# Four PSUM banks for the scores, and the second block's transposes behind the second block's scores, in an attention and Fourier encoder

## The chip, the cores and the metric

The kernel runs on one core of one Trainium2 chip. The metric is device time in microseconds (us), the median of the runs that are given. The engines are named as in the profile: PE multiplies matrices (PEld is its weight load), DVE, ACT and POOL work on vectors, SP issues most transfers. PE writes its results into PSUM, which has eight banks of 2 KB in each of 128 partitions; DVE and ACT read them from there.

## The reference

Two sequences, a prompt of 2048 tokens and a sample of 512, go through two layers and a last normalisation. All of it is float32.

```python
def attention_layer(x, g, w_in, w_out, sink, rel_bias):
    h = rmsnorm(x, g)
    z = h @ w_in                      # q (16 heads of 64), k and v (4 heads), gate
    ...
    o = banded_gqa_with_sink(q, k, v, rel_bias, sink)
    return x + (o * jax.nn.silu(gate)) @ w_out

def banded_gqa_with_sink(q, k, v, rel_bias, sink):
    # blocks of 128 queries against the block before, its own and the one behind (384 keys)
    scores = jnp.einsum('bnqhgd,bnkhd->bnhgqk', qb, kw) * scale + bias
    scores = jnp.where(mask, scores, -jnp.inf)
    ...
    p = jnp.exp(scores - m)
    p = p / (jnp.sum(p, axis=-1, keepdims=True) + jnp.exp(sk - m))
    return jnp.einsum('bnhgqk,bnkhd->bnqhgd', p, vw)

def fourier_layer(x, g, w_gate, w_out):
    f = jnp.fft.fftn(hg, axes=(1, 3), norm="ortho").real   # positions and the channels of a group
    return x + (f * jax.nn.silu(h @ w_gate)) @ w_out
```

## The kernel before

**Numbers.** Each float32 operand of a large product is split into a high and a low part, and a product is three matmuls (`matmul3`, L91 to L94): high by high, high by low, low by high. So nearly every result that PE makes is read twice after it: ACT copies the high part (CAST or COPY), DVE subtracts it from the value to get the low part.

**Chunks.** Attention runs over five chunks of 512 tokens: the sample (called chunk 0 here, `c` in the code), then the four quarters of the prompt (1 to 4). For each chunk `kv_proj` (L299) makes keys (`kwin`) and values (`v`; `vp` is their PSUM bank), with `kh` the keys of one neighbouring block (`halo`), transposed in `kht`. Then a loop of 17 steps, n = 0 to 16 (L842), goes over eight pairs of heads and, for each pair, two pairs of query blocks: step n works at head pair n//2 and blocks 2(n%2) and the next, which are called the first and the second block below. A block at an end of its sequence has 256 keys, any other 384.

**One step.** For the new pair of blocks there are six score matmuls for each block: two heads j = 0 and 1, on the two halves of PE's rows, three products each (`scores`, L467). DVE adds the bias and takes the minimum into SBUF (`biased`, L486, a custom instruction), ACT takes exponentials (`exps`, L494), DVE and ACT divide. For the old pair, that of step n-1, PE transposes the weights of attention, eight or twelve transposes of 64 rows for a block (`transp`, L525), their two halves h = 0 and 1 going into two banks `pt`; ACT and DVE copy them into high and low parts (`parts`, L533 and L534); and PE multiplies them by v (`av`, L551). Between these stand quotas of the projections of q (`qp`) and gate (`gp`) for later heads, and from step 14 on of the output projection (`op`, in `out_proj`). The tile `s` is the gate times its tanh (L414), read from `gp`'s bank, so it frees that bank.

**What sets the order.** The code writes the order of the step by hand. Instructions that go through `pe` or `seq` (L139 to L146) are chained in that order on PE, DVE and ACT; everything else is placed by the scheduler of the tile framework, and an engine runs its instructions strictly in the resulting order. A tile that reuses a bank waits for the last reader of the tile that had it. The diff therefore also moves some instructions that it doesn't mention.

**Banks.** There are eight. Five rotate under the name `bank` (L76) for everything but the scores: pt, av, qp, gp, vp, op, ib. Three fixed ones, spt0 to spt2 (L278), take the scores: the first block's two heads go to spt0 and spt1, the second block's to spt2 and spt0. At step 0 a rotating bank (`fourth`, L840) stands in for the second use of spt0. The first half of the output projection uses spt0 to spt2 and one rotating bank, the second half four rotating ones. The Fourier phase opens a second pool of three banks where the score banks were.

Of the kernel before, what the change touches and what calls it, by code (L numbers as in the profile page):

```python
# [9 lines left out]
F32 = mybir.dt.float32  # L10
# [32 lines left out]
def encoder(  # L43
# [10 lines left out]
    dram = ctx.enter_context(tc.tile_pool(name="dram", bufs=1, space=DRAM))  # L54
    psum = ctx.enter_context(tc.tile_pool(name="psum", bufs=5, space=PSUM))

# [19 lines left out]
    def bank(name):  # L76
        return psum.tile([P, 512], F32, tag="bank", name=name)

# [69 lines left out]
    def attention_phase():  # L148

        with ExitStack() as es:  # L150
# [127 lines left out]
            spt = []  # L278
            for i in range(3):
                spt.append(spsum.tile([P, 512], F32, name=f"spt{i}"))  # L280
# [18 lines left out]
            def kv_proj(c, hs, halo, norms=None, early=None):  # L299
# [33 lines left out]
                if halo:  # L333
                    ps = bank(f"kh{c}")[:, :256]
                    for k in range(KD):
                        matmul3(ps, halo[k], wslice(wk, k, 0, 256), k == 0, k == KD - 1)
                    kh = ap.tile([P, 256], F32, tag="tmp", bufs=2, name=f"kh{c}")
                    ACT.copy(kh, ps)
# [33 lines left out]
                if halo:  # L372
                    pt = bank(f"kht{c}")[:, :256]
                    for t in range(2):
                        PE.transpose(pt[:, t * P : t * P + P], kh[:, t * P : t * P + P], ident)
                        evac_k(t, pt[:, t * P : t * P + P], P, CH + P)
                for t in range(3):
                    zeros(spt[t])
# [50 lines left out]
            def attention(c, p, res, uTs):  # L429
# [82 lines left out]
                def transp(b):  # L512

                    gb, k0, k1 = span(b)
                    ss = [st.pop((b, j)) for j in range(2)]
                    if b % 2 == 0:
                        st["pts"] = ap.tile([P, 2, 2, 3, 2, P], F32R, align_bytes=LINE, tag="pt", bufs=1, name=f"pts{c}_{p}_{b}")
                    ps = st["pt", b] = [
                        bank(f"pt{c}_{p}_{b}_{h}")[:, :384].rearrange("p (k j q) -> p k j q", k=3, j=2) for h in range(2)
                    ]  # L520
                    for j in range(2):
                        for kb in range(k0, k1):
                            for h in range(2):
                                rows = slice(64 * h, 64 * h + 64)
                                pe(PE.transpose(  # L525
                                    ps[h][:, kb, j, :], ss[j][rows, 1 + kb * P : 1 + (kb + 1) * P], ident[rows, rows]
                                ))
# [57 lines left out]
            def out_proj(c, uTs):  # L585
# [4 lines left out]
                def mm(half, k, tiles):  # L590
                    if k == 0 and 3 in tiles:

                        st["ps"] = (spt if half == 0 else []) + [bank(f"op{c}_{half}_{i}") for i in range(3 * (1 - half), 4)]
                    if k % 2 == 0 and 3 in tiles:
# [188 lines left out]
            for c in range(len(CHUNKS)):  # L783
# [55 lines left out]

                fourth = bank(f"s{c}")  # L840
                zeros(fourth)
                for n in range(17):  # L842
# [15 lines left out]
                    if old:  # L858
                        for b in range(2):
                            old[0].transp(old[1] + b)  # L860
                    if new:
                        for j in range(2):
                            new[0].biased(new[1], j)
                        new[0].scores(new[1] + 1, (spt[2], spt[0] if n else fourth))
                    if n == 15:
# [50 lines left out]
    def fourier_phase(tail):  # L916
        with ExitStack() as es:
            fp = es.enter_context(tc.tile_pool(name="four", bufs=1, reuse_waits="tile"))
            psum2 = es.enter_context(tc.tile_pool(name="psum2", bufs=3, space=PSUM, reuse_waits="tile"))

# [272 lines left out]
            for i, s in enumerate(tail):  # L1193
# [7 lines left out]
                if 1 <= i < 9:  # L1201
                    w, k = split_steps[i - 1]
                    take(ready[w, k], k, left, *{"T": ("T2", "T1"), "B": ("B11", "B22")}[w])
            wstack.close()
            zp = es.enter_context(tc.tile_pool(name="zp", bufs=1, side="right", reuse_waits="tile"))

# [567 lines left out]
```

## Time and profile before

| | |
|---|---|
| time, median of 3 runs | 1594.49 us (1594.38 to 1595.07) |
| span of the profiled execution | 1592.8 us |
| its own time beside the span | not listed; the runs lie 1.6 to 2.3 us above this span |
| PE busy | 1581.6 us, 99% |
| PE weight load busy | 1319.4 us, 83% |
| DVE busy | 1145.4 us, 72% |
| ACT busy | 871.7 us, 55% |
| POOL busy | 447.5 us, 28% |

A row of the timeline has the start in us from the start of the span, the length from the first start to the last end in the row, the engine, line, operation, output and inputs, and the count; what stands in brackets at its end is idle time before it. Matmuls overlap, and their ends are modelled, so an engine that waits between two short matmuls is still shown as busy. A stall of PE must be read from the starts of its rows, and from the length of a group against that of a like group.

### The profile page before, as it was taken

Reading aid. Unit: us, or ns where it says so; the run is one execution under the profiler, and the core shown is the slowest. Engines: PE = TensorE matmul, PEld = TensorE weight load, DVE = VectorE, ACT = ScalarE, POOL = GpSimd, SP = SyncE. Lnnn points to the kernel's source line nnn. Section 1 sums busy time; section 2 is a strip of 40 time slices with the busy share of each in tenths; the row PEclk is TensorE's granted clock in tenths of the full one; section 3 lists DMA queues with packets and bytes.
Section 4 is the critical chain, followed back from the end, with each engine's and each line's share of the span. In section 5 each row is a group of like instructions: output and inputs, shape, how many; then the busy total and the mean of one; then the engine's idle time right before and its main releaser. Section 6 shows DMA issues by size and latency. Waiting matters only on the chain. (4 is left out here: it accounts for less than half of the span.)

```text
span 1592.8 us, 27377 instructions
## 1 busy us (share of the span) xinstructions
PE 1581.6 (99%) x9743; PEld 1319.4 (83%) x9743; DVE 1145.4 (72%) x2785; ACT 871.7 (55%) x2088; POOL 447.5 (28%) x613
## 2 busy tenths in 40 slices
PE   9999999999999999999999999999999999999998
PEld 7888888888888888988888888888888888888886
DVE  6788655776547785377764577669778778989896
ACT  6688534776246684257752476646655554343342
POOL 2475642421404314024223242223112111101110
PEclk9999999999999999999999999999999999999999
DMA  7597695566856567656649655675666569557762
GB/s 295 198 342 271 221 361 209 205 235 210 299 208 214 209 235 252 240 198 226 236 168 327 225 205 207 234 255 210 212 209 238 185 218 406 182 186 299 274 207 79
DMA packets 100579, 373.88 MB, mean 235 GB/s; under 512 B 12139, under 2 KB 22379, under 8 KB 83036
## 3 DMA queue, kind: packets, MB, share of 16 engines
q1 hardware_dynamic: 81708, 297.91, 53.0%
q0 software_dynamic: 16400, 70.04, 11.5%
q10 hardware_dynamic: 2336, 4.20, 0.7%
q8 instruction: 77, 1.26, 0.3%
q14 instruction: 58, 0.48, 0.1%
HBM read 280.84 MB, written 91.26 MB: 234 GB/s over the span
## 5 line engine op out<-in xcount | busy, mean ns | idle before, releaser
L486 DVE CUSTOM_DVE_ANT_0 S<-spt,b 128x385 f32<-128x385 f32 (+1 forms) x315 | 154.2, 528 | 128.7 <-PE spt L467 80.2
L94 PE MATMUL gp<-h,wg 128*128 128x512 f32 x960 | 237.4, 395 | 0.0
L94 PE MATMUL qp<-h,wq 128*128 128x512 f32 x960 | 237.0, 396 | 0.0
L533 ACT CAST pts<-pt 128x384 fp32r<-128x384 f32 (+1 forms) x320 | 123.5, 473 | 176.2 <-PE pt L525 176.1
L94 PEld LDWEIGHTS gp<-h,wg 128*128 128x128 f32 x960 | 174.9, 188 | 43.3 <-issue 9.7
L94 PEld LDWEIGHTS qp<-h,wq 128*128 128x128 f32 x960 | 174.9, 188 | 41.2 <-issue 5.5
L494 ACT ACTIVATE S<-S 128x385 f32<-128x385 f32 (+1 forms) x320 | 190.4, 606 | 20.4 <-DVE S L486 17.7
L534 DVE TENSOR_TENSOR pts<-pt,pts 128x384 fp32r<-128x384 f32 (+1 forms) x320 | 147.4, 523 | 21.2 <-ACT pts L533 21.2
L94 PE MATMUL op<-wo,uT 128*128 128x512 f32 x600 | 140.4, 391 | 0.0
L467 PE MATMUL spt<-kwin,qab 64*128 64x384 f32 (+1 forms) x945 | 132.3, 357 | 0.0
L94 PEld LDWEIGHTS op<-wo,uT 128*128 128x128 f32 x600 | 111.9, 188 | 23.9 <-issue 0.7
L575 POOL TENSOR_TENSOR uT<-o,uT 128x256 fp32r<-128x256 f32 x75 | 55.5, 740 | 244.9 <-ACT uT L574 240.6
L551 PEld LDWEIGHTS av<-pts,v 128*128 128x128 f32 x576 | 101.4, 188 | 18.7
L551 PE MATMUL av<-pts,v 128*128 128x512 f32 (+1 forms) x576 | 115.7, 341 | 0.0
L94 PE MATMUL fo<-wo,tTu 128*128 128x512 f32 x480 | 115.2, 392 | 0.0
L467 PEld LDWEIGHTS spt<-kwin,qab 64*128 64x128 f32 x945 | 85.8, 185 | 31.1 <-issue 24.7
L94 PEld LDWEIGHTS fo<-wo,tTu 128*128 128x128 f32 x480 | 88.4, 188 | 17.0
L506 DVE TENSOR_SCALAR S<-S 128x384 f32<-128x384 f32 (+1 forms) x192 | 90.4, 471 | 6.4
L571 POOL TENSOR_TENSOR o<-o,s 128x256 f32<-128x256 f32 x75 | 55.2, 736 | 134.5 <-DVE o L569 134.3
L94 PE MATMUL spt<-wo,uT 128*128 128x512 f32 x360 | 86.7, 392 | 0.0
L94 PEld LDWEIGHTS spt<-wo,uT 128*128 128x128 f32 x360 | 66.5, 188 | 13.7
L525 PEld LDWEIGHTS pt<-ident,S 64*128 64x128 f32 x1792 | 68.0, 138 | 3.7 <-issue 1.8
(321 smaller groups left out, 3030.2 us busy)
## 6 DMA issues: line engine op xcount, KB each, us to landing
wo<-wsd SPq DMA_DIRECT2D x32, 1024.0 KB, 5.7
wq<-wsd SPq DMA_DIRECT2D x31, 1024.0 KB, 7.5
wg<-wsd SPq DMA_DIRECT2D x31, 1024.0 KB, 5.1
x<-x1d SPq DMA_DIRECT2D x40, 512.0 KB, 3.8
b<-b21d SPq DMA_DIRECT2D x40, 512.0 KB, 6.5
b<-rowd SPq DMA_DIRECT2D x40, 384.0 KB, 4.2
xs<-in_x_dram SPq DMA_DIRECT2D x23, 512.0 KB, 6.4
s2d<-gt POOLq DMA_DIRECT2D x40, 256.0 KB, 5.1
```

The source lines that it names most:

```text
L94: pe(PE.matmul(out, a[i], b[j], start=start and i + j == 0, stop=stop and i == 1, skip_group_check=more))
L467: pe(PE.matmul(banks[j][:, 2 + k0 * P : 2 + k1 * P], res["q"][rows, qp, b * P : (b + 1) * P], kwin[g][rows, kp, b * P + k0 * P : b * P + k ...
L486: seq(DVE, DVE.tensor_tensor_reduce(out=s[:, e0:e1], in0=ps[:, 1 + e0 : 1 + e1], in1=st["bias"][:, j, 386 - e1 : 386 - e0][:, ::-1], scale ...
L494: last_exp[0] = seq(ACT, ACT.activation(s[:, e0:e1], s[:, e0:e1], AF.Exp, bias=s[:, 386:387], scale=-1.0, accum_out=s[:, 387:388]))
L506: seq(DVE, DVE.tensor_scalar(s[:, ks], s[:, ks], den, None, ALU.mult))
L525: pe(PE.transpose(ps[h][:, kb, j, :], ss[j][rows, 1 + kb * P : 1 + (kb + 1) * P], ident[rows, rows]))
L533: seq(ACT, ACT.copy(hi, ps[:, k0:k1]))
L534: seq(DVE, DVE.tensor_tensor(lo, ps[:, k0:k1], f32(hi), ALU.subtract))
L551: pe(PE.matmul(to, v, pt, start=n == part == 0, stop=part == 1 and n in (1, len(todo) - 1), skip_group_check=n > 1,))
L571: eng.tensor_tensor(o, o, s, ALU.mult)
L575: low = eng.tensor_tensor(lo, o, f32(hi), ALU.subtract)
```

## The change

It does five things.

1. There are four score banks, spt0 to spt3, and four rotating ones. The second block's scores go to spt2 and spt3.
2. The old pair's second block is transposed behind the new second block's scores, no longer ahead of them. Its half h = 0 goes to a rotating bank, its half h = 1 into spt0 (columns 2 to 385), which the first block's scores of the same step have just used.
3. The halo's keys `kh` are projected into spt3 in place of a rotating bank.
4. The first half of the output projection uses one rotating bank, as its first tile, and spt1 to spt3; the second half three rotating banks and spt0.
5. The rotating pool is closed after the attention's tail, and in the Fourier phase a pool of five takes its place; until then the Fourier phase also has four.

The diff, without what only passes these on:

```diff
-    psum = ctx.enter_context(tc.tile_pool(name="psum", bufs=5, space=PSUM))
+    pstack = ctx.enter_context(ExitStack())
+    banks = [pstack.enter_context(tc.tile_pool(name="psum", bufs=4, space=PSUM))]
...
     def bank(name):
-        return psum.tile([P, 512], F32, tag="bank", name=name)
+        return banks[-1].tile([P, 512], F32, tag="bank", name=name)
...
-            for i in range(3):
+            for i in range(4):
                 spt.append(spsum.tile([P, 512], F32, name=f"spt{i}"))
...
                 if halo:
-                    ps = bank(f"kh{c}")[:, :256]
+                    ps = spt[3][:, :256]
...
-                    ps = st["pt", b] = [
-                        bank(f"pt{c}_{p}_{b}_{h}")[:, :384].rearrange("p (k j q) -> p k j q", k=3, j=2) for h in range(2)
-                    ]
+                    ps = [bank(f"pt{c}_{p}_{b}_{h}")[:, :384] for h in range(2 - b % 2)]
+                    if b % 2:
+                        ps.append(spt[0][:, 2:386])
+                    ps = st["pt", b] = [t.rearrange("p (k j q) -> p k j q", k=3, j=2) for t in ps]
...
-                        st["ps"] = (spt if half == 0 else []) + [bank(f"op{c}_{half}_{i}") for i in range(3 * (1 - half), 4)]
+                        own = [bank(f"op{c}_{half}_{i}") for i in range(3 if half else 1)]
+                        st["ps"] = own + spt[:1] if half else spt[1:] + own
...
-                fourth = bank(f"s{c}")
-                zeros(fourth)
...
                     if old:
-                        for b in range(2):
-                            old[0].transp(old[1] + b)
+                        old[0].transp(old[1])
                     if new:
                         for j in range(2):
                             new[0].biased(new[1], j)
-                        new[0].scores(new[1] + 1, (spt[2], spt[0] if n else fourth))
+                        new[0].scores(new[1] + 1, spt[2:])
+                    if old:
+                        old[0].transp(old[1] + 1)
...
-            psum2 = es.enter_context(tc.tile_pool(name="psum2", bufs=3, space=PSUM, reuse_waits="tile"))
+            psum2 = es.enter_context(tc.tile_pool(name="psum2", bufs=3, space=PSUM, side="right", reuse_waits="tile"))
...
             wstack.close()
+            pstack.close()
+            banks.append(es.enter_context(tc.tile_pool(name="psum3", bufs=5, space=PSUM, reuse_waits="tile")))
```

Three places of the order show what moves. In a name such as pt2_3_2_0_6578 the numbers are chunk, head pair, block and half, and a number that the build gives. The line numbers of the changed kernel are one or two higher.

The first place is PE at step 8 of chunk 2, with the scores of head pair 4 and the transposes of head pair 3. Before:

```order
L467 MATMUL spt0_227<-kwin_230,qab2_4_6534 128x384
L467 MATMUL spt1_228<-kwin_230,qab2_4_6534 128x384
...
L525 MATMUL pt2_3_2_0_6578<-ident_72,S2_3_2_0_6486 128x64
L525 MATMUL pt2_3_2_1_6579<-ident_72,S2_3_2_0_6486 128x64
...
L525 MATMUL pt2_3_3_0_6592<-ident_72,S2_3_3_0_6508 128x64
L525 MATMUL pt2_3_3_1_6593<-ident_72,S2_3_3_0_6508 128x64
...
L467 MATMUL spt2_229<-kwin_230,qab2_4_6534 128x384
L467 MATMUL spt0_227<-kwin_230,qab2_4_6534 128x384
...
L94 MATMUL gp2_4_6555<-h2_4_5150,wg2_4_6193 128x512 x3
```

The same place in the changed kernel:

```order
L468 MATMUL spt0_227<-kwin_231,qab2_4_6489 128x384
L468 MATMUL spt1_228<-kwin_231,qab2_4_6489 128x384
...
L527 MATMUL pt2_3_2_0_6533<-ident_72,S2_3_2_0_6428 128x64
L527 MATMUL pt2_3_2_1_6534<-ident_72,S2_3_2_0_6428 128x64
...
L468 MATMUL spt2_229<-kwin_231,qab2_4_6489 128x384
L468 MATMUL spt3_230<-kwin_231,qab2_4_6489 128x384
...
L527 MATMUL pt2_3_3_0_6557<-ident_72,S2_3_3_0_6463 128x64
L527 MATMUL spt0_227<-ident_72,S2_3_3_0_6463 128x64
...
L95 MATMUL gp2_4_6510<-h2_4_5115,wg2_4_6151 128x512 x3
```

The twelve transposes of the second block (3) now stand between the second block's scores and the projection, and their second half writes spt0.

The second place is PE at step 14 of chunk 2, where the output projection begins; the names in brackets are the engines and transfers that an instruction waits for. Before:

```order
L195 MATMUL ib3_4_7412<-ident_72,inv3_7172 128x128 [waits PE_49]
L94 MATMUL op2_0_3_7415<-wo2_0_0_7416,uT2_0_5574 128x512 [waits DMAHW0_49,PE_49]
L94 MATMUL op2_0_3_7415<-wo2_0_0_7416,uT2_0_5574 128x512 x2
L94 MATMUL op2_0_3_7415<-wo2_0_0_7416,uT2_1_5626 128x512 x3
L94 MATMUL op2_0_3_7415<-wo2_0_2_7424,uT2_2_5820 128x512 [waits DMAHW4_49]
```

The same place in the changed kernel:

```order
L196 MATMUL ib3_4_7360<-ident_72,inv3_7122 128x128 [waits PE_49]
L95 MATMUL op2_0_0_7363<-wo2_0_0_7364,uT2_0_5539 128x512 [waits DMAHW5_49,DVE_49]
L95 MATMUL op2_0_0_7363<-wo2_0_0_7364,uT2_0_5539 128x512 x2
L95 MATMUL op2_0_0_7363<-wo2_0_0_7364,uT2_1_5588 128x512 x3
L95 MATMUL op2_0_0_7363<-wo2_0_2_7372,uT2_2_5781 128x512 [waits DMAHW4_49]
```

The order is the same, but the first matmul of the output projection now waits for DVE: with four rotating banks it gets the bank of the last gate projection, which DVE frees when it writes `s` (L414). It is so in chunks 0, 1 and 2.

The third place is DVE in the steps 2, 6, 10 and 14 of chunks 1 to 3, here step 2 of chunk 2, where the last two blocks of one head's keys are copied to the front of `kwin` for the next chunk (L306), once the scores that read the front are done. Before:

```order
L534 TENSOR_TENSOR pts2_0_2_5827<-pt2_0_3_1_5843,pts2_0_2_5827 128x6x64
L486 ISA S2_1_1_0_5878<-spt2_229,b2_1_5624 128x385
...
L486 ISA S2_1_1_1_5880<-spt0_227,b2_1_5624 128x385
...
L502 RECIPROCAL S2_1_0_0_5856<-S2_1_0_0_5856 128x1
L306 CAST kwin_230<-kwin_230 128x2x256
L506 TENSOR_SCALAR S2_1_0_0_5856<-S2_1_0_0_5856 128x384
```

The same place in the changed kernel:

```order
L536 TENSOR_TENSOR pts2_0_2_5788<-pt2_0_2_1_5790,pts2_0_2_5788 128x6x64
L307 CAST kwin_231<-kwin_231 128x2x256
L536 TENSOR_TENSOR pts2_0_2_5788<-pt2_0_3_0_5813,pts2_0_2_5788 128x6x64
L536 TENSOR_TENSOR pts2_0_2_5788<-spt0_227,pts2_0_2_5788 128x6x64
L487 ISA S2_1_1_0_5838<-spt2_229,b2_1_5586 128x385
...
L487 ISA S2_1_1_1_5840<-spt3_230,b2_1_5586 128x385
```

The copy of the keys has moved up: it stands ahead of the copies of the second block's transposes and of the second block's biased scores, where it stood behind both.

More of the change, by code (lines that the diff above doesn't have):

```diff
@@ L376, in kv_proj @@
                         evac_k(t, pt[:, t * P : t * P + P], P, CH + P)
-                for t in range(3):
+                for t in range(4):
                     zeros(spt[t])
```

## Prediction

> **What bounds the kernel now.** I read the page's table of busy times first, then PE's waits, then the timeline of single steps, since the table cannot show a short stall.
>
> ```profile
> PE 1581.6 (99%) x9743; PEld 1319.4 (83%) x9743; DVE 1145.4 (72%) x2785; ACT 871.7 (55%) x2088; POOL 447.5 (28%) x613
> ...
> PE idle L239 <- DVE idle L236: 1.2, 1, 1.2
> PE W L94 <- DVE c L1136: 1.0, 1, 1.0
> ```
>
> PE is busy 99% of a span of 1592.8 us, and its longest visible waits are 1.2 and 1.0 us, once each. So PE is the bound, and what the change is worth must be sought inside the time in which PE counts as busy. One step of chunk 3 (n = 4), PE first, then DVE:
>
> ```profile
> 715.03 0.78 PE L467 MATMUL spt<-kwin,qab 64*128 64x384 f32 x6
> 715.66 0.90 PE L525 MATMUL pt<-ident,S 64*128 64x64 f32 x24
> 716.37 0.99 PE L467 MATMUL spt<-kwin,qab 64*128 64x384 f32 x6
> 717.28 0.96 PE L94 MATMUL gp<-h,wg 128*128 128x512 f32 x3
> ...
> 715.95 0.56 DVE L486 CUSTOM_DVE_ANT_0 S<-spt,b 128x385 f32<-128x385 f32 x1 [2.00 <-issue]
> 716.43 0.55 DVE L486 CUSTOM_DVE_ANT_0 S<-spt,b 128x385 f32<-128x385 f32 x1
> ...
> 715.03 0.44 PE L467 MATMUL spt<-kwin,qab 64*128 64x384 f32 x2
> ...
> 716.37 0.64 PE L467 MATMUL spt<-kwin,qab 64*128 64x384 f32 x2
> ```
>
> The first block's six score matmuls take 0.78 us, the second block's, of the same shape, 0.99. The last two rows, from narrow windows, show why: the first two matmuls of the first block (heads 0 and 1 on the two halves of PE's rows) lie within 0.44 us, those of the second within 0.64. The second of these writes spt0, which DVE still reads: its first biased instruction ends at 715.95 + 0.56 = 716.51, and a 0.44 us matmul that ends at 716.37 + 0.64 = 717.01 starts at 716.57, so 0.06 us after the release. This is a stall of 0.2 us that the page counts as busy.
>
> **The change part by part.**
>
> *Removed: the stall in the second scores.* A group of six without a stall takes 0.78 us at 384 keys and 0.62 at 256 (the 91.56 row, a first block). The seven kinds of step, second blocks at 83.95 and below:
>
> ```profile
> 91.56 0.62 PE L467 MATMUL spt<-kwin,qab 64*128 64x256 f32 x6
> ...
> 83.95 0.84 PE L467 MATMUL spt<-kwin,qab 64*128 64x256 f32 x6
> 92.61 0.98 PE L467 MATMUL spt<-kwin,qab 64*128 64x384 f32 x6
> 297.01 1.02 PE L467 MATMUL spt<-kwin,qab 64*128 64x384 f32 x6
> 305.96 0.85 PE L467 MATMUL spt<-kwin,qab 64*128 64x384 f32 x6
> 725.69 0.89 PE L467 MATMUL spt<-kwin,qab 64*128 64x384 f32 x6
> 934.47 0.71 PE L467 MATMUL spt<-kwin,qab 64*128 64x256 f32 x6
> 943.43 1.11 PE L467 MATMUL spt<-kwin,qab 64*128 64x384 f32 x6
> ```
>
> A chunk has 8 odd and 7 even steps with both groups. Chunk 0: 8 x (0.84 - 0.62) + 7 x (0.98 - 0.78) = 3.2. Chunk 1: 8 x 0.24 + 7 x 0.07 = 2.4. Chunks 2 and 3, by 725.69 and 716.37: 8 x 0.11 + 7 x 0.21 = 2.35 each. Chunk 4: 8 x 0.09 + 7 x 0.33 = 3.0. The sum is 13.3. With spt2 and spt3 neither head waits, as their last readers are a whole step back: all of it goes, **-13.3 us**.
>
> *Added: a wait in the moved transposes.* The second block's transposes now write spt0 and wait for the same biased instruction. What counts is how much later PE gets there. The transposes' own work is unchanged, so I build the new time from rows.
>
> ```profile
> 82.73 0.79 PE L467 MATMUL spt<-kwin,qab 64*128 64x384 f32 x6
> 83.35 0.79 PE L525 MATMUL pt<-ident,S 64*128 64x64 f32 x20
> 92.02 0.79 PE L525 MATMUL pt<-ident,S 64*128 64x64 f32 x20
> 83.55 0.56 DVE L486 CUSTOM_DVE_ANT_0 S<-spt,b 128x385 f32<-128x385 f32 x1 [1.42 <-PE spt L467]
> 725.17 0.56 DVE L486 CUSTOM_DVE_ANT_0 S<-spt,b 128x385 f32<-128x385 f32 x1 [1.89 <-PE spt L467]
> ```
>
> From transposes to second scores 20 take 83.95 - 83.35 = 0.60 and 24 take 716.37 - 715.66 = 0.71, so a pair costs 0.055: 12 take 0.71 - 6 x 0.055 = 0.38, 8 take 0.60 - 6 x 0.055 = 0.27. Six scores take 83.35 - 82.73 = 0.62 to the next transposes at 384 keys, 92.02 - 91.56 = 0.46 at 256. Odd steps of chunk 0 (8 transposes, then 256 keys) reach spt0 at 83.35 + 0.27 + 0.46 = 84.08, and it is free at 83.55 + 0.56 + 0.06 = 84.17: 0.09 late, eight times, 0.7 us. The step at 715.03 reaches it at 715.66 + 0.38 + 0.62 = 716.66, free at 716.57: 0.09 to spare. An odd step of chunk 2 or 3 reaches it at 725.69 - 12/2 x 0.055 + 0.62 = 725.98, free at 725.79. So 67 of 75 steps have at most some 0.2 us to spare, and a matmul whose release comes just ahead may lose part of its weight load's lead, which no row shows. Bounds: 0.7 (nothing more) and 13.3 (the stall moves over whole). I take the end that the rows are near to, with 0.025 for each of the 67 steps: **+2.4 us**.
>
> *The move itself.* The same matmuls run with one more change from scores to transposes; the matching joints are paid today, scores to transposes, transposes to scores. Taken as 0; bounded by one transposed pair a step either way, 75 x 0.055 = 4. The copies of these transposes come 0.6 to 0.7 us later on ACT and DVE, and the product with v that reads them stands behind twelve projection matmuls, three of which take 0.96 us: that is the cover.
>
> *Added: the output projection's first bank.* In chunks 0, 1 and 2 its first matmul now waits for `s`, the DVE reading of the last gate.
>
> ```profile
> 167.09 0.49 PE L94 MATMUL op<-wo,uT 128*128 128x512 f32 x1
> 167.71 0.69 DVE L414 SCALAR_TENSOR_TENSOR s<-th,gp 128x512 f32<-128x512 f32 x1 [0.27 <-ACT th L412]
> ...
> 383.58 0.94 PE L94 MATMUL op<-wo,uT 128*128 128x512 f32 x3
> 383.42 0.69 DVE L414 SCALAR_TENSOR_TENSOR s<-th,gp 128x512 f32<-128x512 f32 x1
> ...
> 598.98 1.40 PE L94 MATMUL op<-wo,uT 128*128 128x512 f32 x5
> 599.07 0.69 DVE L414 SCALAR_TENSOR_TENSOR s<-th,gp 128x512 f32<-128x512 f32 x1 [0.19 <-ACT th L412]
> ...
> L306 DVE CAST kwin<-kwin x12: 592/622/641, 273.2 to 812.6; 128x512 fp32r<-128x512 f32 x12
> ```
>
> Before, `s` ended 168.40 - 167.09 = 1.31, 0.53 and 0.78 us after that matmul's start; with 0.06 for the release, 2.8 us of PE standing still, and behind the waiting matmul stand all of PE's later ones. Two things make it later: the copy of keys (0.62 us) now stands ahead of the second block's softmax, and so of `s`, in chunks 1 and 2, and PE arrives earlier by that step's own stall, while the softmax does not (0.20, 0.07, 0.20). That gives up to 1.7 more, 4.5 in all; if DVE's idle time absorbs the copy, 2.8 to 3.3. DVE is in one unbroken row there, so I take **+4.3 us**.
>
> *Added: waits between chunks.* With four rotating banks the first q bank of chunks 0, 2 and 3 comes from a v bank that DVE frees with its low part.
>
> ```profile
> 31.12 0.40 PE L94 MATMUL qp<-h,wq 128*128 128x512 f32 x1
> 31.14 0.46 DVE L367 SCALAR_TENSOR_TENSOR v<-vp,vsc,v 128x256 fp32r<-128x256 f32 x1
> ...
> 456.05 0.49 PE L94 MATMUL qp<-h,wq 128*128 128x512 f32 x1
> 455.55 0.79 DVE L367 SCALAR_TENSOR_TENSOR v<-vp,v 128x256 fp32r<-128x256 f32 x2 [8.72 <-ACT v L366]
> ```
>
> Chunk 0: 31.60 + 0.06 - 31.12 = 0.54. Chunk 2: the second low part ends at 456.34, 0.35 after PE's start with the release; chunk 3 the same. **+1.3 us** with small change; 0 if the scheduler's order lets PE do something else, at most double if a further bank is late.
>
> *Added: the start of the Fourier phase*, whose first transposes (trb) take the banks of the output projection's last tiles.
>
> ```profile
> 1070.38 0.27 PE L998 MATMUL trb<-ident,x 128*128 128x128 f32 x1
> 1069.22 1.37 DVE L632 TENSOR_TENSOR xr<-xr,op 128x512 f32<-128x512 f32 x2
> 1070.58 0.69 DVE L632 TENSOR_TENSOR xrl<-xrl,op 128x512 f32<-128x512 f32 x1
> ```
>
> The first bank is free at 1070.59, the second at 1071.27, 0.27 and (four transposes on) some 0.4 us after PE would be there: **+0.4 us**, between 0.2 and 0.6.
>
> *Moved by the scheduler in chunk 0:* four roundings of q and gate weights on ACT now stand ahead of copies and exponentials.
>
> ```profile
> 29.35 1.05 ACT L120 CAST wq<-w32q 128x1024 fp32r<-128x1024 f32 x1 [0.16 <-DMA w32q<-in_w_in_dram]
> ```
>
> Each is 1.05 us; at most 4.2 if all four fall on PE's path, nothing if ACT, at 55%, has room. I take **+0.8**. Two bias loads are moved behind x loads on SP's queue, most of a step ahead of their use: 0. The removed `fourth` bank and its two small memsets cost nothing, as DVE does them between steps.
>
> *Sum:* -13.3 + 2.4 + 4.3 + 1.3 + 0.4 + 0.8 = -4.1. The span of 1592.8 becomes 1588.7; the runs lie 1.7 above this span at their median, so 1594.5 - 4.1 = **1590.4 us**, 0.26% faster. A difference under 0.2%, 3.2 us, is taken as no change.
>
> **The rivals.**
>
> *A, the stall moves over (slower).* Place: the first transpose into spt0, in each step. Its price is what j = 1 pays now if weights queued behind the waiting matmul also come late. The other additions make 6.8, so the change stops paying at 6.5 of wait, 0.09 a step, and is slower by over 3.2 us from 9.7 on, 0.13 a step. At 0.15, 11.3 us: 1594.5 - 13.3 + 6.8 + 11.3 = 1599.3. For it: 0.09 us late in chunk 0, and 0.09 to spare at 715.03. Against it: the stalled second scores start 0.06 us after their release and then run on. The Trainium skill speaks for A (Perfetto Trace Analysis, Matmuls): independent groups of matmuls should rotate through different banks, so that one is evacuated while the next is written, and spt0 now serves scores and transposes in one step. By that rule alone the 2.4 would go towards the 11.3; the rows at 725 give it 0.19 us of room, so I leave it the smaller chance. Chance 0.18.
>
> *B, the new waits are hidden.* The output projection's and the chunks' waits could vanish, if `s` moves up with PE and DVE's order. Then -13.3 + 2.4 + 1.0 = -9.9: 1584.6. For it: PE's stall ends earlier on every step, so DVE gets its gate bank earlier too. Against it: at 167.71 DVE waits for ACT, not for a bank. The same page (Optimization Strategy) says that a gap repeated over a stretch of the saturated engine can mean that PSUM is short for the next tile. The 0.2 us at 716.37, in 75 steps, agree; by it alone the four banks would bring 13.3 and B would be the case. Chance 0.14.
>
> *C, within 0.2%.* Copies of keys and weight roundings delay more than counted: ACT's four at 4.2, `s` at 4.5, waits of transposes at 4: -13.3 + 4 + 4.5 + 1.6 + 0.5 + 4.2 = +1.5, or half of that excess: 1593.2. Chance 0.28.
>
> *The forecast,* 1587 to 1591.3, has 0.40.
>
> **How the numbers follow.** Faster is B, the forecast and none of C: 0.54; C gives 0.28 for no change, A 0.18 for slower. The range leaves out the deep end of B (under 1586) and the far end of A (over 1597): 1586.0 to 1597.0. The forecast's own range is 1587 to 1591.3.
>
> **What the changed kernel's profile would show.** Right, if the second scores at 384 keys take 0.78 us in every step, and a transposed second block follows with a length near the present; if the first op matmul of chunks 0 to 2 starts just after `s`, with idle time of over 1 us ahead of it that is put down to DVE; and if the first q matmul of chunks 0, 2 and 3 waits 0.3 to 0.5 us. Wrong, if the transposes into spt0 spread over 0.1 us more than their pairs need in most steps (A), if op starts without a wait (B), or if a step of chunk 0 shows PE waiting for ACT's copies (C). What I cannot see from here is how much of a weight load's lead a late release costs.

## The result: no measurable change

The changed kernel takes 1595.26 us (median of 12 runs, 1592.86 to 1598.92), the kernel before 1595.07 (12 runs, 1594.38 to 1597.30). The ratio is 1.0003, with a 95% interval from 0.9994 to 1.0011: no change that can be told from none. The forecast was 1590.4; case C, within 0.2%, is what came. The profiled execution has a span of 1595.8 us. It took 1597.6 us, 2.3 over the median, while the span of the kernel before belongs to an execution near its median, so losses that are read from these two traces are larger than those in the medians.

First PE's busy time on the page of the changed kernel, then its list of PE's waits (what waits, for what: us in total, times, longest):

```profile
PE 1576.0 (99%) x9743; PEld 1320.9 (83%) x9743; DVE 1152.2 (72%) x2785; ACT 875.0 (55%) x2088; POOL 446.9 (28%) x613
```

```profile
PE op L95 <- DVE s L415: 3.0, 3, 1.5
PE z L95 <- DVE z L1072: 1.6, 2, 1.3
PE Ap L95 <- ACT gp L1306: 1.4, 1, 1.4
PE idle L240 <- DVE idle L237: 1.2, 1, 1.2
PE av L553 <- DVE pts L536: 1.0, 3, 0.3
PE W L95 <- DVE c L1138: 1.0, 1, 1.0
PE spt L95 <- ACT h L218: 1.0, 1, 1.0
```

PE's busy time fell by 5.6 us while the span grew by 3.0: stalls that had been counted as busy went, and waits that the page can see came. The new ones are op for `s`, av (the product with v) for its copies, and z and Ap in the Fourier phase; the one of spt for h stands in a second trace of the kernel before as well (the last experiment).

The timeline of the changed kernel at the step that the prediction read (chunk 3, n = 4), PE, then DVE:

```profile
718.18 0.79 PE L468 MATMUL spt<-kwin,qab 64*128 64x384 f32 x6
718.80 0.54 PE L527 MATMUL pt<-ident,S 64*128 64x64 f32 x12
719.15 0.77 PE L468 MATMUL spt<-kwin,qab 64*128 64x384 f32 x6
719.75 0.22 PE L527 MATMUL pt<-ident,S 64*128 64x64 f32 x1
719.76 0.24 PE L527 MATMUL spt<-ident,S 64*128 64x64 f32 x1
...
720.24 0.72 PE L95 MATMUL gp<-h,wg 128*128 128x512 f32 x2
...
719.10 0.56 DVE L487 CUSTOM_DVE_ANT_0 S<-spt,b 128x385 f32<-128x385 f32 x1 [1.73 <-issue]
```

The second scores now take 0.77 us where they took 0.99. DVE frees spt0 at 719.10 + 0.56 + 0.06 = 719.72, the transposes get there at 719.76 and do not wait. From first scores to projection the step took 717.28 - 715.03 = 2.25 us, now 720.24 - 718.18 = 2.06. Added up in the same way over the 75 steps, from the start of the first scores to the start of the projection, it is 158.4 us before and 148.5 now: 9.9 us gained. So the change does in its own place what it says, and the gain is given back elsewhere.

Where it is given back is read from the start of each step against the same step of the kernel before. In the first profile of the changed kernel: 0.7 us late at the first step of chunk 0, and 0.34 lost ahead of the first q matmul in each of chunks 2 and 3; 1.6 lost in steps 7 and 8 of chunk 0, of which 0.7 lies inside step 8 and so in the sum of 148.5 already; 3.8 at step 14 of chunks 0, 1 and 2 (1.75, 0.95, 1.15, where op begins); 2.8 at steps 11 and 12 of chunk 2 and step 11 of chunk 3. With small pieces that makes nearly the 9.9 again: at the last step of chunk 4 it stands 0.25 us ahead of the kernel before, and the Fourier phase, in which no instruction has moved, then loses 3.3 us in three places.

### The profile page after: what moved, and what is told of

It is laid out like the page before. It is cut to its first block, busy times and chain, and to the rows that moved or that the text cites. A ratio compares the mean times of both kernels' runs of the same rounds, so it can differ in the third digit from the quotient of the medians.

```text
span 1595.8 us, 27413 instructions
## 1 busy us (share of the span) xinstructions
PE 1576.0 (99%) x9743; PEld 1320.9 (83%) x9743; DVE 1152.2 (72%) x2785; ACT 875.0 (55%) x2088; POOL 446.9 (28%) x613
## 5 line engine op out<-in xcount | busy, mean ns | idle before, releaser
L535 ACT CAST pts<-pt 128x384 fp32r<-128x384 f32 (+1 forms) x240 | 100.4, 462 | 171.5 <-PE pt L527 163.9
L536 DVE TENSOR_TENSOR pts<-pt,pts 128x384 fp32r<-128x384 f32 (+1 forms) x240 | 114.6, 523 | 27.7 <-ACT pts L535 27.6
L95 PE MATMUL op<-wo,uT 128*128 128x512 f32 x480 | 119.0, 392 | 3.0 <-DVE s L415 3.0
L95 PE MATMUL spt<-wo,uT 128*128 128x512 f32 x480 | 120.4, 391 | 0.0
L468 PE MATMUL spt<-kwin,qab 64*128 64x384 f32 (+1 forms) x960 | 118.5, 352 | 0.0
L95 PEld LDWEIGHTS op<-wo,uT 128*128 128x128 f32 x480 | 89.3, 188 | 22.3 <-DVE s L415 3.8
L95 PEld LDWEIGHTS spt<-wo,uT 128*128 128x128 f32 x480 | 89.1, 188 | 18.4
L507 DVE TENSOR_SCALAR S<-S 128x384 f32<-128x384 f32 (+1 forms) x192 | 97.8, 510 | 6.8
L468 PEld LDWEIGHTS spt<-kwin,qab 64*128 64x128 f32 x960 | 74.6, 186 | 28.4 <-issue 27.5
L527 PE MATMUL pt<-ident,S 64*128 64x64 f32 x1344 | 82.6, 222 | 0.0
```

The lines of the kernel that those rows point to most:

```text
L95: pe(PE.matmul(out, a[i], b[j], start=start and i + j == 0, stop=stop and i == 1, skip_group_check=more))
L468: pe(PE.matmul(banks[j][:, 2 + k0 * P : 2 + k1 * P], res["q"][rows, qp, b * P : (b + 1) * P], kwin[g][rows, kp, b * P + k0 * P : b * P + k ...
L507: seq(DVE, DVE.tensor_scalar(s[:, ks], s[:, ks], den, None, ALU.mult))
L527: pe(PE.transpose(ps[h][:, kb, j, :], ss[j][rows, 1 + kb * P : 1 + (kb + 1) * P], ident[rows, rows]))
L535: seq(ACT, ACT.copy(hi, ps[:, k0:k1]))
L536: seq(DVE, DVE.tensor_tensor(lo, ps[:, k0:k1], f32(hi), ALU.subtract))
```

## Experiments

All were timed beside the kernel before on the same chip, whose medians there were 1595.5 to 1596.0 us. There were three chips: one for the first four experiments, one for the next four, one for the last two; where medians of different chips are compared, it is said. Theory: each place is a wait of PE of its own, in the order of a queue or of banks, and can be mended apart. Rival: PE is held by something that does not care for these orders (the softmax's row of work on DVE and ACT, or chance), so a mended wait comes back elsewhere.

**The changed kernel again**, unaltered.

> The changed kernel once more, unaltered. In the first profile of it the attention ends (step 15 of chunk 4) 0.25 us earlier than before, and the Fourier phase then loses 3.2 us in three waits of PE (1.3 us for DVE's z, 0.4, and 1.4 us for ACT's gp), though no instruction is in another place there. Theory: those three come from the time at which transfers land and are chance, so this profile has other ones or none, its attention again ends within 1 us of before, and the median lies within 1 us of before (1594 to 1596). Rival: the five banks of the Fourier phase's new pool make PE wait there, so the same two waits of over 1 us stand at the same instructions again (the z transform of about 1181 us, the Ap product of about 1503 us), and the loss of 3 us is the change's own.

Measured: 1596.04 us (11 runs, 1593.65 to 1601.57), ratio 1.0002 (0.9993 to 1.0011). The attention phase ends 0.76 us later than before. Its losses stand at the same places, but one has another size: step 11 of chunk 2 loses 3.6 us, not 1.1. Two things make it larger:

```profile
572.84 4.46 PE L95 MATMUL gp<-h,wg 128*128 128x512 f32 x12
...
572.80:574.00 1.20, 1.20 (x5) 0.50 0.98 410
```

PE's product with v waits 1.17 us there, not 0.23. Behind it the granted clock of PE (in the second row, from a table of stretches, the 0.50) is 0.50 for 3.4 us, and twelve gate matmuls take 4.46 us, where 2.91 is usual. So 1.5 of the 3.6 us is not a wait. In the traces of this case such a stretch appears, beside the end of each span, only once more, at the 8.0 us wait of the kernel with the transposes in spt1; the 2.8 us wait of op in the kernel with the moved roundings has none, so no rule for it follows from here. In the Fourier phase the z wait came again, 1.1 us late against before (1.5 the first time), the Ap wait with 0.5 (1.4). Neither expectation holds whole: the median and the end of the attention are where the theory has them, but the waits are at the same instructions again, with other sizes. The second trace of the kernel before, further down, says more.

**The bank of the output projection.** The norms' broadcasts (ib) leave the rotating banks.

```diff
-                    ps = bank(f"ib{c}_{i0}") if place is None else place
+                    ps = place[i0 // 4]
...
-                            invb = spread(c + 1, inv)
+                            invb = spread(c + 1, inv, spt[:1:-1])
+                            for t in spt[2:]:
+                                zeros(t)
```

> As the changed kernel, but the two broadcasts of the next chunk's norms (ib, at step 14) go into spt3 and spt2, whose zero columns are then written again, so the output projection's first bank is one that DVE freed long ago. Theory (the op wait is PE's own loss): the three waits of op for s, 3.0 us of visible idle time and about 3.8 us in the starts, are gone, nothing comes in their place, and the time falls by 3 to 4.5 us against the changed kernel, to 1590.5 to 1592.5. Rival (PE is held by DVE's row of softmax there, so that the wait only moves on): op starts at once, but the transposes or products of step 15 wait for their copies by as much, and the time stays within 1 us of the changed kernel.

Measured: 1590.59 us (7 runs), ratio 0.9969 (0.9958 to 0.9980); 5.5 us less than the changed kernel's 1596.04 on the same chip. PE and DVE at step 14 of chunk 0, first in the changed kernel:

```profile
167.56 0.71 PE L196 MATMUL ib<-ident,inv 128*128 128x128 f32 x5
169.81 1.88 PE L95 MATMUL op<-wo,uT 128*128 128x512 f32 x7 [1.55 <-DVE s L415]
...
169.07 0.69 DVE L415 SCALAR_TENSOR_TENSOR s<-th,gp 128x512 f32<-128x512 f32 x1 [0.27 <-ACT th L413]
```

then with the broadcasts in score banks:

```profile
166.86 0.71 PE L196 MATMUL spt<-ident,inv 128*128 128x128 f32 x5
167.33 1.87 PE L95 MATMUL op<-wo,uT 128*128 128x512 f32 x7
...
168.11 0.69 DVE L415 SCALAR_TENSOR_TENSOR s<-th,gp 128x512 f32<-128x512 f32 x1 [0.24 <-ACT th L413]
```

op starts 0.8 us ahead of `s`, and nothing behind it waits in its place: the starts of step 15 no longer lose 1.75, 0.95 and 1.15 us. So the theory holds for this wait, 3.8 us; the rest of the 5.5 us in the medians I can't place, beyond that steps 11 and 12 (next) lose 1.6 us in this profile and 4.3 in the one of the changed kernel beside it.

**The order of SP's loads.**

```diff
-            SP.dma_start(f32(w), f32(wsd[n]))
+            after(SP.dma_start(f32(w), f32(wsd[n])), last_x[0] if n > 11 else None)
...
-                        after(SP.dma_start(xs[i], x[tok + i * P : tok + (i + 1) * P, :]), last_exp[0])
+                        last_x[0] = SP.dma_start(xs[i], x[tok + i * P : tok + (i + 1) * P, :])
+                        after(last_x[0], last_exp[0])
```

> As the changed kernel, but the weight loads of the last gate and of the output projection stay behind the x loads on SP's queue in chunks 1 to 4, as they stood before. Theory: in chunks 2 and 3 ACT waits up to 2.9 us for an x load whose square stands ahead of its copies of the transposes, and PE's product with v waits behind that; with the old order steps 11 and 12 of chunk 2 and step 11 of chunk 3 lose their 0.5 to 1.0 us each, some 2.4 us in all, and the time falls by 1.5 to 3 us against the changed kernel. Rival: x lands late by chance in that one profile, the order of the queue does not matter, and the time stays within 0.8 us of the changed kernel.

Measured: 1593.55 us (11 runs), ratio 0.9986 (0.9977 to 0.9995), 2.5 us less than the changed kernel. SP's issues (SPq), ACT and PE in step 11 of chunk 2, in the changed kernel:

```profile
560.84 0.32 SPq L117 DMA_DIRECT2D wg<-wsd  x1
561.51 0.81 SPq L177 DMA_DIRECT2D xs<-in_x_dram  x2
...
567.33 1.06 ACT L169 ACTIVATE xs<-xs 128x1024 f32<-128x1024 f32 x1 [2.92 <-DMA xs<-in_x_dram]
568.50 1.24 ACT L535 CAST pts<-pt 128x384 fp32r<-128x384 f32 x3
...
570.18 0.50 PE L553 MATMUL av<-pts,v 128*128 128x512 f32 x1 [0.23 <-ACT pts L535]
571.02 1.42 PE L553 MATMUL av<-pts,v 128*128 128x512 f32 x7 [0.33 <-DVE pts L536]
```

in the kernel before:

```profile
554.39 2.44 SPq L176 DMA_DIRECT2D xs<-in_x_dram  x2
560.22 0.33 SPq L116 DMA_DIRECT2D wg<-wsd  x1
...
569.26 1.54 PE L551 MATMUL av<-pts,v 128*128 128x512 f32 x8
```

and in the changed kernel with the old order of the loads:

```profile
555.38 1.86 SPq L177 DMA_DIRECT2D xs<-in_x_dram  x2
560.32 0.33 SPq L117 DMA_DIRECT2D wg<-wsd  x1
...
563.79 1.05 ACT L169 ACTIVATE xs<-xs 128x1024 f32<-128x1024 f32 x1
...
569.23 1.54 PE L554 MATMUL av<-pts,v 128*128 128x512 f32 x8
```

In the changed kernel the gate's weights are issued ahead of two x loads. SP issues in order and the weights wait for a buffer, which PE's gate matmuls free, until 560.84. So the first of the two x loads, which goes out at 555.38 with the old order, goes out at 561.51, 6.1 us later. ACT stands 2.92 us before the square of that x, and behind the square stand the copies of the transposes, for which av waits. Steps 11 of chunks 2 and 3 lose nothing with the old order. One loss of 1.1 us stayed at step 12 of chunk 2, where ACT waited 3.0 us for a later x load. In the kernel before ACT waits 2.0 us at that place, and PE loses nothing; the two loads were issued at the same time (569.5 and 569.4 us), so when a load lands varies beside the order.

**The weight roundings of chunk 0.** For head pairs 5 to 7 the loads are called behind the first block's exponentials, and ACT's rounding is ordered behind them.

```diff
-        ACT.copy(w[:, 0], w32)
+        after(ACT.copy(w[:, 0], w32), last_cast[0])
...
+                    if c == 0 and n in (7, 9, 11):
+                        last_cast[0] = last_exp[0]
+                        loads[n // 2 + 2]()
+                        last_cast[0] = None
```

> As the changed kernel, but in chunk 0 ACT rounds the q and gate weights of head pairs 5 to 7 behind the exponentials of a step's first block, no longer among its copies of the transposes. Theory: PE's 1.4 us of loss in steps 7 and 8 of chunk 0 (a product with v of 1.63 us where 1.14 is usual, transposes of 0.76 us where 0.34 is) come from two such roundings of 1.05 us, and go: 1.0 to 1.6 us faster than the changed kernel. Rival: the roundings are only moved from the copies into the softmax, which is then late for the next step's transposes, and the time is the same within 0.5 us or worse.

Measured: 1599.26 us (11 runs), ratio 1.0024 (1.0015 to 1.0033), slower than the changed kernel by 3.2. The loss of steps 7 and 8 is gone (step 9 starts 0.1 us ahead of the kernel before, not 1.4 late), so the roundings among the copies were its cause. (In the changed kernel there are two of them in step 7, and the second waits 0.67 us for its own load.) But steps 12 to 14 lose 5.5 us, where the changed kernel loses 1.3. SP's issues, then ACT there:

```profile
142.22 14.75 SPq L100 DMA_DIRECT2D w32o<-in_w_out_dram  x5
157.34 0.53 SPq L438 DMA_DIRECT2D b<-rowd  x1
...
165.67 0.20 ACT L450 COPY b<-sk 128x4 f32<-128x4 f32 x1 [4.46 <-DMA b<-rowd]
165.89 1.14 ACT L535 CAST pts<-pt 128x384 fp32r<-128x384 f32 x3
```

The same in the changed kernel:

```profile
142.40 11.75 SPq L100 DMA_DIRECT2D w32o<-in_w_out_dram  x3
157.28 0.38 SPq L438 DMA_DIRECT2D b<-rowd  x1
...
162.85 0.20 ACT L450 COPY b<-sk 128x4 f32<-128x4 f32 x1 [1.70 <-DMA b<-rowd]
```

SP's issues had moved again. The bias load of head pair 7 goes out at the same time, 157.3, but the last load of output weights ahead of it is issued until 156.97, where it was 154.15, and the bias is there 2.8 us later. The small copy into its tile stands on ACT ahead of the copies of the transposes. As with x, a load that comes late holds up ACT's row; here it was not issued later. That the weights' transfer slowed it is likely, and not shown.

**Two mends together**, the bank and the order of the loads.

> As the changed kernel, with both mends that gained: the norms' broadcasts in spt3 and spt2, and the old order of SP's loads. Theory (each wait is a loss of PE of its own): the gains add, 5.2 and 2.3 us in the medians, so some 7.5 us less than the changed kernel, 1587.5 to 1589.5, and the profile shows neither a wait of op for s nor a step of chunks 2 and 3 that is late by over 0.3 us. Rival (they share a cause, DVE's and ACT's row at the end of a chunk): together they bring little more than the larger one, 1590 to 1592.

Measured: 1589.27 us (5 runs), ratio 0.9958 (0.9944 to 0.9971). It is 6.3 us less than the kernel before beside it; the changed kernel, on another chip, was 0.2 above. So some 6.5 us came of the 8.0 that the two brought apart (5.5 and 2.5): most of the sum, and within intervals of some 2 us either way the whole; both losses are gone from the trace. Inside chunks 1 to 3 no step loses 0.3 us, and op has no wait; what is left are 0.35 us each at the starts of chunks 2 and 3, and 1.4 at that of chunk 0 in this trace.

**The two mends, the roundings, and the bias load, which was meant to go ahead of the output weights.**

> As the one before, with chunk 0's weight roundings behind the exponentials once more, and the bias load of head pair 7 kept ahead of the output weights on SP's queue, since ACT waited 4.5 us for it when only the roundings were moved. Theory: the 1.4 us of steps 7 and 8 of chunk 0 go and nothing comes back at steps 13 and 14, 1.0 to 1.6 us less than with the two mends. Rival: the output weights now land late, so that step 14 of chunk 0 waits for them, and the time is the same or higher.

Measured: 1591.53 us (10 runs), ratio 0.9975 (0.9966 to 0.9985), 2.3 us more than without the last two edits. Steps 7 and 8 are mended again, and steps 12 to 14 lose 2.9 us. The time is the rival's, its mechanism is not: PE shows no wait for output weights. SP and ACT there:

```profile
157.62 0.54 SPq L441 DMA_DIRECT2D b<-rowd  x1
...
166.31 0.20 ACT L454 COPY b<-sk 128x4 f32<-128x4 f32 x1 [4.84 <-DMA b<-rowd]
```

The edit did not do what it was meant to. The bias load of head pair 7 still goes out at 157.6, behind six loads of output weights, and ACT waits 4.84 us for it, as it waited 4.46 in the kernel with the roundings alone. So whether the moved roundings pay once this load is early stays untested.

**Only the order changed**: five rotating banks and three for the scores, but the second block's transposes behind its scores.

```diff
-                        for b in range(2):
-                            old[0].transp(old[1] + b)
+                        old[0].transp(old[1])
...
                         new[0].scores(new[1] + 1, (spt[2], spt[0] if n else fourth))
+                    if old:
+                        old[0].transp(old[1] + 1)
```

> The kernel before with only the order changed: five rotating banks, three for the scores, the second block's scores in spt2 and spt0, but its transposes behind them and in rotating banks. Theory (what a score or transpose into spt0 pays is the time from PE's arrival to the end of the biased instruction): PE now comes to the second scores 0.34 us earlier, with 12 transposes ahead of them, or 0.22 with 8, and waits that much less the same work longer; the stall grows from 0.2 to some 0.55 us a step, 25 to 30 us more than before in 75 steps, 1619 to 1626. Rival (the stall belongs to the change of work on PE, not to the bank): within 4 us of before.

Measured: 1625.05 us in one run. From first scores to projection the 75 steps take 185.2 us, 26.8 more than before. A step of chunk 2:

```profile
512.71 0.42 PE L467 MATMUL spt<-kwin,qab 64*128 64x384 f32 x1
513.29 0.79 PE L467 MATMUL spt<-kwin,qab 64*128 64x384 f32 x5 [0.16 <-DVE S L486]
```

The second head now starts 0.58 us behind the first, where it was 0.20 in such steps. Without the fourth score bank the order costs 30 us in all. The opposite half, four score banks with the transposes left in place, wasn't tried: with four rotating banks, the four halves of transposes have no room while a projection holds a bank.

**The transposes in spt1**, which DVE frees later.

```diff
-                        ps.append(spt[0][:, 2:386])
+                        ps.append(spt[1][:, 2:386])
...
-                        st["ps"] = own + spt[:1] if half else spt[1:] + own
+                        st["ps"] = own + spt[1:2] if half else spt[:1] + spt[2:] + own
```

> As the changed kernel, but the second block's second half of transposes goes into spt1, which DVE frees with its second biased instruction, 0.48 us (0.35 at 256 keys) after spt0; the output projection's halves take spt0 and spt1 in exchanged roles. Theory: arrival is unchanged and the release is later, so the wait is the difference: 0.61 and 0.16 us in odd and even steps of chunk 0, 0.47 and 0.16 in chunk 1, 0.33 and 0.43 in chunks 2 and 3, 0.52 and 0.43 in chunk 4, in all 29 us more than the changed kernel, 1621 to 1628. Rival (a late release also costs the lead of the weight loads, some 0.1 us a step more): 1630 to 1635. Second rival (PE has other work to do there): under 10 us more.

Measured: 1634.31 us in one run. Over the 75 steps it is 179.3 us, 30.8 more than the changed kernel's 148.5, by the theory 29. The time lies in the first rival's range, and outside the theory's, for another reason: the exchange of the output projection's banks made PE wait 8.0 us once at the end of chunk 0, and the granted clock was 0.50 for 5.6 us behind it, 10.9 us in the starts, which I hadn't counted. Without it the time would be some 1623.4. PE in a step of chunk 2:

```profile
504.97 0.21 PE L527 MATMUL pt<-ident,S 64*128 64x64 f32 x1
505.43 0.27 PE L527 MATMUL spt<-ident,S 64*128 64x64 f32 x1 [0.24 <-DVE S L487]
505.43 0.28 PE L527 MATMUL pt<-ident,S 64*128 64x64 f32 x1
505.54 0.22 PE L527 MATMUL spt<-ident,S 64*128 64x64 f32 x1
505.60 0.22 PE L527 MATMUL spt<-ident,S 64*128 64x64 f32 x1
```

The wait is arrival to release, as the theory says; after it one pair takes 0.11 us where the next take 0.06. So a late release costs some 0.05 us of lead, not 0.1.

**The mended kernel with a value projection in a score bank.**

```diff
-                    ps = [bank(f"vp{c}_{i0}_{i}")[:, :256] for i in range(len(group))]
+                    ps = [bank(f"vp{c}_{i0}_{i}")[:, :256] for i in range(min(len(group), 3))]
+                    if len(group) == 4:
+                        ps.append(spt[0 if c else 3][:, :256])
```

> As the kernel with the two mends that gained, and the fourth value projection of a group goes into a score bank that is idle there (spt3 in chunk 0, spt0 in the others), so that four banks are left for three of them. Theory (the first q matmul of chunks 0, 2 and 3 waits for a bank): 0.3 to 0.6 us come back at each of three starts, 1.0 to 1.4 us less than with the two mends. Rival (PE then waits at its next step of these starts, for the keys or for the norms, as DVE's and ACT's row is the same): within 0.6 us of the two mends.

Measured: 1587.40 us (5 runs, 1586.19 to 1588.78), ratio 0.9943 (0.9929 to 0.9957), 1.9 us less than the two mends alone, which ran on another chip; against the kernel before beside each it is 8.6 and 6.3, so 2.4. The first q matmul of chunk 0, in the changed kernel and here:

```profile
31.75 0.50 PE L95 MATMUL qp<-h,wq 128*128 128x512 f32 x1 [0.20 <-DVE v L368]
```

```profile
31.08 1.09 PE L95 MATMUL qp<-h,wq 128*128 128x512 f32 x4
```

Step 1 of chunk 0 now starts with the kernel before, and so do the first q matmuls of chunks 2 and 3, counted from the last step of the chunk before, where the changed kernel lost 0.34 us each. This kernel beats both, by 0.57% the kernel before. At the last step of chunk 4 its trace is 8.8 us ahead of before, at the end of the span 6.2: the Fourier phase takes 2.6 us more in it.

**The kernel before again**, for its trace.

> The kernel before once more, for its trace. Question: are the waits of PE in the Fourier phase (z near 1180 us, Ap near 1500 us) that the changed kernel shows and the first trace of the kernel before does not a matter of chance? Theory: this trace has some of them too, 0.4 us or more against the first trace of the same kernel, and the attention phase lies within 0.5 us of the first trace's. Rival: none of them is there, and both traces of before agree within 0.3 us in the Fourier phase, so that the changed kernels' 0.4 to 1.4 us there are the change's own.

One run, 1595.23 us. Three of PE's waits in its trace, the first and the last from the attention phase:

```profile
PE spt L94 <- ACT h L217: 1.0, 1, 1.0
PE Ap L94 <- ACT gp L1302: 0.5, 1, 0.5
PE pt L525 <- ACT wq L120: 0.3, 1, 0.3
```

The Ap wait is there, 0.55 us against the first trace of the same kernel, so part of what the changed kernels show differs between executions of one kernel. The z wait is not: it is in both traces of the changed kernel (1.5 and 1.1 us), and at 0.8, 0.4 and 0.3 us or not at all in those of the other versions. In the changed kernel:

```profile
1180.85 1.70 PE L95 MATMUL z<-chan_sb,tTb 128*128 128x256 f32 x12 [1.33 <-DVE z L1072]
...
1503.61 0.39 PE L95 MATMUL Ap<-gp,tbp 128*128 128x260 f32 x1 [1.35 <-ACT gp L1306]
```

No instruction stands elsewhere there. From the last step of chunk 4 to the end, the two traces of the changed kernel take 3.3 and 1.7 us more than the first of the kernel before, its other versions 0.2 to 2.6, and this second trace of the kernel before 0.2. Whether these waits belong to the time at which the changed kernel reaches the phase, or to chance, stays open.

The last of the three waits is one more thing: in step 8 of chunk 0 a rounding of q weights holds up the transposes in the kernel before too, and costs it 0.50 us in this trace, nothing in the first. Against this trace the 75 steps gain 10.5 us, not 9.9.

## Why the prediction was right and where it was wrong

The range held the time, and the forecast of 4.1 us faster failed. That the range held is the merit of its width: the loss by the x loads was in none of its terms or rivals. The terms of the attention's inner loop came out; one step beside it did not. Point by point:

- *Removed stall and the wait in the moved transposes, -13.3 + 2.4 = -10.9.* Measured -9.9 against the first trace of the kernel before, -10.5 against the second. The removed part is 14.1 in the lengths of the second scores, and the wait came out near its total, but only in part at its place: in odd steps of chunk 0 the last transposes take 0.68 us from their start to the projection's where 0.46 is usual, in odd steps of chunk 4 0.55, 2.5 us in all, and little elsewhere. The sum had 0.7 in chunk 0 and 0.025 in every other step, so that its 2.4 fits is partly luck. The only-order and spt1 kernels show the rule behind it, arrival against release: 26.8 us where 25 to 30 was expected, and 30.8 where 29 was.
- *The output projection's bank, +4.3.* 3.8 in the starts. The mechanism and its three places were right. It was a matter of two broadcast banks, as moving these alone ended it.
- *Between chunks, +1.3.* 0.7 or 0.4 us at chunk 0 in the two traces, and 0.34 to 0.37 at each of chunks 2 and 3, so 1.4 and 1.1: the term was right. The mend brought 1.9 in the medians, or 2.4 by the kernel before beside each, with intervals of 2 us on each.
- *The Fourier start, +0.4.* The first transposes wait 0.2 us, and the products behind them make it up: 0.
- *Chunk 0's roundings, +0.8.* 1.6 us in the first trace of the changed kernel, in chunk 0 as named, since two roundings among the copies of step 7 delay av and, behind it, the transposes of step 8. Some 0.5 of it the kernel before can have too, as its second trace shows.
- *SP's queue, 0.* This is the step that failed. The prediction looked at the bias loads that move back in the queue, and took them as harmless. What matters is what moved ahead of x: the gate's weights wait for their buffer on SP, and the first x load behind them goes out 6.1 us later. The square of x stands on ACT ahead of the copies of the transposes, and nothing of that is in a sum of PE's terms. Steps 11 and 12 of chunks 2 and 3 lost 2.8 and 4.3 us in two traces of the changed kernel (1.5 of the 4.3 by the half clock) and 1.1 with the old order; in the medians the order is worth 2.5. With 2.8 for it and 1.6 for the roundings, -4.1 becomes -0.5, where the attention of the first trace ends at -0.25, and inside the interval of the medians (-1.0 to +1.8). What the Fourier phase adds is not in this sum, and its cause is open.

Of the rivals, A is refuted in its price: the weight loads' lead is 0.05 us for a wait, and only the 16 odd steps of chunks 0 and 4, and four single ones, wait by more than 0.05. B is refuted by op's 3.0 us of visible idle time. C named the roundings and `s`, not the x loads.

The Trainium skill's rule that independent groups of matmuls should rotate through different banks (Perfetto Trace Analysis, Matmuls) agrees with the spt1 run, where sharing a bank a little too soon cost 0.4 us a step; with spt0 the sharing costs little, as the release comes nearly in time.

## What to carry to other kernels

When a change moves work in a hand-written order, the scheduler moves loads as well: compare every queue's order, and for each load that falls back follow the first instruction that needs it to what stands behind that on its in-order engine. A stall inside short matmuls is not seen as idle here; a gain there must be read from starts. The bank taken from the rotating pool was paid where a long holder met a new successor (the last gate, then the output projection), so look for which new pairing of holder and successor arises before the pool is cut.

## What was not expected

One step of the same program lost 1.1 us in one trace and 3.6 in another, with the same order of everything, in part because the granted clock fell to 0.50 behind the longer wait; and the changed kernel's runs spread over 6 to 8 us where the kernel before spreads over 3. With the loads in the old order and op's bank free, five runs lay within 1.3 us; five others, with the value projection moved as well, within 2.6. The slowest run of the changed kernel, 1601.57 us, has a mean granted clock of 0.996 where most have 0.998 or 0.999, so a stretch of half clock may lie in it too; it has no trace.
